# Two-block kernel: where the mixers' weights get their lower parts

## The chip, the cores and the metric

The kernel runs on 1 core of one Trainium2 chip. The metric is the device time of one execution in microseconds. A core has TensorE (PE, with its weight loads PEld), VectorE (DVE), ScalarE (ACT), GpSimd (POOL) and SyncE (SP), each with a queue of its own that it works through in order, and 16 DMA engines that move what any of the queues issues. Times of the profile are microseconds from the start of the span unless they are marked ns.

## The reference

Two transformer blocks follow each other on 512 tokens of width 1024, in float32. Each has an FFN, a mixer and a second FFN, with RMS norms and residuals around them. The first block prepends 16 meta tokens (528 columns).

```python
def first_block(...):
    h = concat(meta, x)
    h = h + 0.5 * rmsnorm(swiglu(rmsnorm(h, gn[0]), ffn_w_in[0], ffn_w_out[0]), gn[1])
    u = rmsnorm(h, gn[2])
    y = mlstm_mixer(u, a_w_in, a_conv_w, a_conv_b, a_gate_b, a_w_out)     # mixer A
    h = h + rmsnorm(y, gn[3])
    ...
def second_block(...):
    ...
    proj = rms_norm(h, mix_norm) @ w_in                                   # mixer B
    a = mla_group(c_q, c_kv, k_pe, pos_f, q_norm, w_uq, kv_norm, w_ukv)
    r = retention_group(r_q, r_k, r_v, r_g, pos_f, decay_fwd, decay_bwd)
    h = h + concat(a, r) @ w_o
    ...
```

Mixer A is an mLSTM: a causal convolution over queries and keys, gates, a scan, output gates and `a_w_out` (1024x1024). Mixer B joins a latent attention with 8 heads (`w_uq`, `w_ukv`) and a two-sided retention with 8 heads, and ends in `w_o` (1024x1024).

## The kernel before

Every float32 product is made of three: a matrix is split into an upper part `hi`, rounded to float32r, and a lower part `lo` = value - `hi`; TensorE multiplies hi by hi, hi by lo and lo by hi and adds them up in PSUM (`mm`, L484). Activations are split as they come (`split`, L463 to L470); weights are split when they have been loaded.

The class `Weights` runs the weights' way. SP loads raw weights into two buffers `raw0` and `raw1` in turn (`load`, L85 to L99). `pump` (L107) takes the next unit, 128 partitions by 1024 columns as a rule, gives it a free slot (a pair of tiles `hi`, `lo`), lets ACT write `hi` (L120) and lets `lo_engine` subtract it from the raw weights into `lo` (L121). When the last unit of a raw buffer is split, the load of the raw weights after the next ones is issued into it (L127 to L128); on the chip SP waits until the readers of the buffer are done. `take` hands units to TensorE in order, `free` and `release` give slots back and call `pump` again. In mixer A there are six slots, in mixer B four.

`lo_engine` is DVE in the FFNs and POOL in the two mixers: set to POOL at L1129 (mixer A, after its first items) and L1339 (mixer B), and back to DVE in `Bridge.tail` and near the end of mixer B. In mixer A a unit is one head's or one pair's columns of `a_w_in`, then `a_w_out` in raw loads of two units each (256 columns, so a unit reads eight runs of 512 bytes per partition). In mixer B a unit is 128 columns of `w_in_2` or, once for each pair of heads, the `w_uq` and `w_ukv` columns of `add_mla`, which come in four pieces (96, 16 and 16 columns of four blocks, and 256 columns). `w_o_2` follows.

Around this the mixers run items: an item multiplies one unit with all tokens, and `evac` brings the sums out of PSUM with DVE. Steps of the attention are laid between an item's matmuls (`run_mm`, `run_item`). In mixer A, `done_gate` runs a chain on DVE (L1005 to L1027: a polynomial at L1015, scans, an exponential on ACT), `item_qk.done` the convolution (three taps at L1067, a last product at L1070), `masked` scales the scores (L1177) and splits them, and `divided` makes the quotient (L1205 to L1212). In mixer B, `newton` (L380 to L387) makes the inverse roots of the norms, `Rms.to` the diagonal matrices (L450) that TensorE turns into rows (L451), `item_rqk` the rotated queries and keys (L1525 to L1536), and `ret_attn` multiplies them (L1589).

POOL has other work in the mixers: the masks of mixer A (L1158), copies and one subtraction for queries and keys (L1080, L1081, L1539), and a few DMAs. In the FFNs POOL issues accumulating DMAs of 256 KB (L95), which add weights in HBM to a raw tile.

Of the kernel before, what the change touches and what calls it, by code (L numbers as in the profile page):

```python
# [8 lines left out]
F32 = mybir.dt.float32  # L9
F32R = mybir.dt.float32r  # L10
I32 = mybir.dt.int32
ACTF = mybir.ActivationFunctionType
ALU = mybir.AluOpType
# [50 lines left out]
class Weights:  # L64
# [42 lines left out]
    def pump(self):  # L107
        nc = self.nc
        while self.n_split < len(self.subs):
            r, make, half = self.subs[self.n_split]  # L110
            if self.hold and self.raws[r][2] and self.raws[r][1] == 5:
                break
            idle = self.idle_halves if half else self.idle
            if not idle:
                break
            slot = idle.pop(0)
            self.dma(r + 1)
            unit, splits = make(self.raw_tiles[r], slot.hi, slot.lo)
            for ho, lw, src in splits:
                nc.scalar.copy(out=ho, in_=src)  # L120
                self.lo_engine.tensor_tensor(out=lw, in0=src, in1=ho.bitcast(F32), op=ALU.subtract)  # L121
            unit.slot = slot
            self.units.append(unit)
            self.n_split += 1
            self.raws[r][1] -= 1
            if self.raws[r][1] == 0:
                del self.raw_tiles[r]  # L127
            if self.raws[r][1] == 0:  # L128
                self.dma(r + 3)
            if self.raws[r][2] and self.raws[r][1] == 2 and self.n_raw == r + 2 and self.raws[r + 2][2]:  # L130
                self.load(r + 2, True)
# [88 lines left out]
def two_blocks(ctx: ExitStack, tc, d, out):  # L220
    nc = tc.nc
    pe, act, dve, pool = nc.tensor, nc.scalar, nc.vector, nc.gpsimd

    def open_pool(name, bufs=1, **kw):
        cm = tc.tile_pool(name=name, bufs=bufs, reuse_waits="tile", **kw)
        return cm, cm.__enter__()
# [30 lines left out]
    def cut(t, k, sl):  # L257
        return t[:, k, sl[0]:sl[0] + sl[1]]


    W = Weights(nc, rawp)
# [316 lines left out]
    def run_lead(items, br, keep=None):  # L578

        sa, sb = br.sa, br.sb  # L580
        us = [W.take(it.units) for it in items]
        if keep:
            W.reserve(keep, 1)
        accA = [[ps("accA")[0:u.hi.shape[2], 0:sa[1]] for u in uu] for uu in us]

        pairs = [(u, p) for uu, aa in zip(us, accA) for u, p in zip(uu, aa)]
        step = br.first
        for i in range(0, len(pairs), step):
            for k in ALLK:
                for u, p in pairs[i:i + step]:  # L590
                    mm([(p, sa)], u, [k], NORMED, last=KD - 1)
                if i == 0 and k == br.ks[0]:
                    br.pres[sa].flush(1)
                    br.post_b()
                elif i == 0 and k == br.ks[1]:
                    br.set_rp(sb)
        br.pres[sa].compact()
        for c in range(KD):
            br.chunk(c, sb)
        held = []  # L600
        for i, it in enumerate(items):
            bank = ps("accB")
            accB = [bank[0:u.hi.shape[2], n * sb[1]:(n + 1) * sb[1]] for n, u in enumerate(us[i])]
            for n, (u, p) in enumerate(zip(us[i], accB)):
                for k in ALLK:
                    mm([(p, sb)], u, [k], NORMED, last=KD - 1)
                    br.pres[sb].flush(KD - 1 - k)
                if i == 0 and n == 0:
                    br.pres[sa].set_r()
                    for x, a in zip(items, accA):  # L610
                        x.evac(sa, a)
            held.append(accB)
            if i == 0:
                br.pres[sb].compact()
            if i == 2:
                br.pres[sb].set_r()
            while i >= 2 and held:
                x = items[i + 1 - len(held)]
                x.evac(sb, held.pop(0))
                if x.done:  # L620
                    x.done()
                W.free(x.units)
# [503 lines left out]
    make = {"k": lambda n: item_qk("k", n), "q": lambda n: item_qk("q", n), "v": item_v, "o": item_o}  # L1126
    lead = [Item(1, ev_gate, done_gate)] + [make[k](n) for k, n in order[:3]]
    run_lead(lead, br)
    W.lo_engine = pool  # L1129
    for k, n in order[3:6]:  # L1130
        run_item(make[k](n), AB)
    cm_s, sp = open_pool("mixs")
# [203 lines left out]
    close_pool(cm_w2)  # L1336


    W.lo_engine = pool  # L1339
    cm_b, bp = open_pool("mixb")  # L1340
    hsp = drp.tile([P, KD, SEQ], F32, name="hsp")
    pool.dma_start(out=hsp, in_=h[:, :, NM:TT])
# [415 lines left out]
    for sl in halves:  # L1758
        for c in range(KD):
# [14 lines left out]
            src = cut(h, c, sl)  # L1774
# [57 lines left out]
```

## Time and profile before

| | |
|---|---|
| median of 3 runs | 2091.21 us (2089.55 to 2098.18) |
| profiled execution | 2091.01 us, span 2089.1 us, mean granted clock 0.99 |
| PE busy | 2006.3 us (96%) |
| DVE busy | 1549.0 us (74%) |
| ACT busy | 1027.4 us (49%) |
| POOL busy | 326.9 us (16%) |
| HBM read | 230.53 MB |

The share of busy time is an average over stages with different limits, and a busy TensorE is not one at its peak, since ends of matmuls are modelled. A row of a timeline gives the start, the duration, the engine, the line, the operation, what is written and read, and in brackets the idle time of the engine just before, with what ended it.

### The profile page before, as it was taken

What the parts mean: (1) busy time and instruction counts of PE and PEld (TensorE: products, weight loads), DVE (VectorE), ACT (ScalarE), POOL (GpSimd) and SP (SyncE); (2) the same over time, 40 slices, a digit from 0 to 9 for tenths busy, and PEclk for the clock granted to TensorE, in tenths of its full rate; (3) what the DMA queues carried; (4) which work ended last, traced back from release to release, by engine and by line L of the source; (5) the groups of instructions that cost most, each with busy time, mean ns of one, the idle gap of its engine ahead of it and who ended that gap; (6) DMA issues with size and microseconds to landing.
All of it is one profiled execution on the core that took longest, in us unless ns stands there. A gap on an engine that the chain in (4) does not pass through costs nothing.

```text
span 2089.1 us, 34858 instructions
## 1 busy us (share of the span) xinstructions
PE 2006.3 (96%) x13583; PEld 1840.6 (88%) x13583; DVE 1549.0 (74%) x2949; ACT 1027.4 (49%) x1973; POOL 326.9 (16%) x290
## 2 busy tenths in 40 slices
PE   8999999989999999999999999998999999999998
PEld 8999999988889989989998988987777778898998
DVE  6848477787886767758777775877888877676684
ACT  5445255445555445436443543654666643353462
POOL 0011020034430002011000201103222100010200
PEclk9999999999999999999999999999999999999999
DMA  6357565222223327567532766733112153475661
GB/s 186 96 111 152 147 140 135 72 77 81 87 81 110 79 79 156 145 137 146 162 80 77 154 152 137 148 118 104 47 47 61 41 141 100 107 158 133 147 151 55
DMA packets 387851, 237.01 MB, mean 113 GB/s; under 512 B 10427, under 2 KB 383926, under 8 KB 387686
## 3 DMA queue, kind: packets, MB, share of 16 engines
q1 hardware_dynamic: 317446, 192.94, 31.4%
q0 software_dynamic: 69680, 40.62, 14.1%
q8 instruction: 106, 1.74, 0.3%
q10 hardware_dynamic: 560, 1.24, 0.2%
q14 instruction: 59, 0.48, 0.1%
HBM read 230.53 MB, written 4.23 MB: 112 GB/s over the span
## 4 chain that ended last, share of the span: by engine, by line
PE 77%; DVE 12%; ACT 5%; issue 3%; POOL 1%; DMA 1%; ACTq 0%; POOLq 0%; DVEq 0%
PE dn L484 23%; PE sa L696 17%; PE acc L484 11%; PE sc L696 8%; PE sb L696 4%; PE accB L484 3%; PE accA L484 3%; PE wo L484 2%; DVE wlo L121 1%; DVE accF L1206 1%; ACT sqFalse L753 1%; PE p L419 1%; PE ro L1604 1%; ACT whi L120 1%; DVE cv L1067 1%
## 5 line engine op out<-in xcount | busy, mean ns | idle before, releaser
L120 ACT CAST whi<-raw 128x1024 fp32r<-128x1024 f32 (+3 forms) x500 | 392.8, 801 | 360.0 <-PE dn L484 163.2
L121 DVE TENSOR_TENSOR wlo<-raw,whi 128x512 fp32r<-128x512 f32 (+2 forms) x456 | 402.3, 905 | 112.9 <-ACT whi L120 110.4
L484 PE MATMUL dn<-gh,whi 128*128 128x256 f32 (+2 forms) x908 | 277.6, 326 | 0.5 <-ACT gh L465 0.5
L484 PE MATMUL dn<-gl,whi 128*128 128x256 f32 (+2 forms) x908 | 277.7, 326 | 0.0
L484 PE MATMUL dn<-gh,wlo 128*128 128x256 f32 (+2 forms) x908 | 276.9, 325 | 0.0
L484 PE MATMUL acc<-nh,whi 128*128 128x512 f32 (+2 forms) x600 | 196.4, 361 | 8.9 <-DVE y L1212 3.9
L484 PE MATMUL acc<-nl,whi 128*128 128x512 f32 (+2 forms) x600 | 192.0, 355 | 0.0
L484 PE MATMUL acc<-nh,wlo 128*128 128x512 f32 (+2 forms) x600 | 191.6, 354 | 0.0
L484 PEld LDWEIGHTS dn<-gh,whi 128*128 128x128 f32 x908 | 163.0, 188 | 16.5 <-ACT gh L465 0.7
L484 PEld LDWEIGHTS dn<-gh,wlo 128*128 128x128 f32 x908 | 163.1, 188 | 15.0
L484 PEld LDWEIGHTS dn<-gl,whi 128*128 128x128 f32 x908 | 163.0, 188 | 15.1
L696 PE MATMUL sa<-nh,whi 128*128 128x256 f32 (+1 forms) x488 | 142.5, 292 | 24.9 <-ACT sqFalse L753 24.9
L696 PE MATMUL sc<-nh,wlo 128*128 128x256 f32 (+1 forms) x488 | 137.4, 282 | 0.0
L696 PE MATMUL sa<-nh,wlo 128*128 128x256 f32 (+1 forms) x488 | 137.3, 281 | 0.0
L696 PE MATMUL sc<-nh,whi 128*128 128x256 f32 (+1 forms) x488 | 137.2, 281 | 0.0
L696 PE MATMUL sa<-nl,whi 128*128 128x256 f32 (+1 forms) x488 | 137.1, 281 | 0.0
L696 PE MATMUL sc<-nl,whi 128*128 128x256 f32 (+1 forms) x488 | 137.0, 281 | 0.0
L484 PEld LDWEIGHTS acc<-nh,whi 128*128 128x128 f32 (+1 forms) x600 | 108.1, 194 | 25.9 <-DVE z L1054 4.5
L696 PEld LDWEIGHTS sa<-nh,whi 128*128 128x128 f32 x488 | 91.8, 188 | 34.9 <-ACT sqFalse L753 34.7
L484 PEld LDWEIGHTS acc<-nh,wlo 128*128 128x128 f32 (+1 forms) x600 | 107.0, 194 | 15.5
L484 PEld LDWEIGHTS acc<-nl,whi 128*128 128x128 f32 (+1 forms) x600 | 106.8, 193 | 13.9
L95 POOL DMA_DIRECT2D raw<-in_ffn_w_up x32 | 41.1, 1285 | 455.9 <-DMA raw<-in_ffn_w_up 245.4
(492 smaller groups left out, 5569.5 us busy)
## 6 DMA issues: line engine op xcount, KB each, us to landing
raw<-in_ffn_w_in SPq DMA_DIRECT2D x56, 512.0 KB, 3.9
raw<-in_ffn_w_gate SPq DMA_DIRECT2D x44, 512.0 KB, 3.7
raw<-in_ffn_w_in SPq DMA_DIRECT2D x64, 256.0 KB, 3.2
raw<-in_ffn_w_out SPq DMA_DIRECT2D x16, 1024.0 KB, 7.7
raw<-in_ffn_w_up SPq DMA_DIRECT2D x64, 256.0 KB, 3.3
raw<-in_ffn_w_down SPq DMA_DIRECT2D x16, 1024.0 KB, 7.2
raw<-in_a_w_in SPq DMA_DIRECT2D x18, 512.0 KB, 3.6
rawx<-in_ffn_w_in SPq DMA_DIRECT2D x32, 256.0 KB
```

The lines of the kernel that those rows point to most:

```text
L95: self.nc.gpsimd.dma_start(out=dst(t), in_=src, accum_op=ALU.add)
L120: nc.scalar.copy(out=ho, in_=src)
L121: self.lo_engine.tensor_tensor(out=lw, in0=src, in1=ho.bitcast(F32), op=ALU.subtract)
L419: pe.matmul(self.p1[:, self.n:self.n + 2], lhsT=src[:, o:o + P], rhs=ones[:, 0:2], start=True, stop=True)
L484: pe.matmul(p, lhsT=w[:, k], rhs=cut(x, k, sl), start=(k == 0 and j == 0), stop=(k == last and j == 2))
L696: pe.matmul(acc, lhsT=w[:, 4 * i + k], rhs=x[:, k], start=start and k == 0 and j == 0, stop=k == 3 and j == 2, skip_group_check=not start)
L753: last = act.copy(out=m3, in_=o.a)
L1067: dve.scalar_tensor_tensor(out=v, in0=z[:, t0 + j:t0 + j + n], scalar=col(V_CW + 8 * j + c), in1=v, op0=ALU.mult, op1=ALU.add)
L1206: dve.reciprocal(out=dn, in_=dn)
L1604: pe.matmul(o[i], lhsT=vt_[:, i, j], rhs=s_[i, j][b], start=(j == 0 and b == 0), stop=(j == 3 and b == 1))
```

## The change

In the two mixers the lower part is no longer subtracted by POOL. ACT writes the negated upper part into `lo` (a copy with scale -1, rounded to float32r as `hi` is), and a DMA that POOL's queue issues adds the raw weights to it, from SBUF to SBUF. The FFNs, the tail of mixer A and the end of mixer B keep DVE's subtraction. The places at which the way is switched are the same as before.

```diff
@@ in Weights.pump
             for ho, lw, src in splits:
                 nc.scalar.copy(out=ho, in_=src)
-                self.lo_engine.tensor_tensor(out=lw, in0=src, in1=ho.bitcast(F32), op=ALU.subtract)
+                if self.lo_engine is None:
+                    nc.scalar.activation(out=lw, in_=src, func=ACTF.Copy, scale=-1.0)
+                    nc.gpsimd.dma_start(out=lw.bitcast(F32), in_=src, accum_op=ALU.add)
+                else:
+                    self.lo_engine.tensor_tensor(out=lw, in0=src, in1=ho.bitcast(F32), op=ALU.subtract)
@@ in mixer A, after run_lead
-    W.lo_engine = pool
+    W.lo_engine = None
@@ at the head of mixer B
-    W.lo_engine = pool
+    W.lo_engine = None
```

## Rows read from the trace of the kernel before

**Rows 1.** The page's first line.

```profile
span 2089.1 us, 34858 instructions
```

**Rows 2.** The table of stretches: start and end, length, then busy time and instructions of PE, PEld, DVE, ACT and POOL, the granted clock, the DMA engines' share and GB/s. The first two lie in mixer A, the last at the end of mixer B.

```profile
436.00:460.00 24.00, 17.07 (x116) 15.90 (x115) 23.46 (x23) 8.08 (x14) 11.63 (x8) 0.86 0.24 67
...
520.00:600.00 80.00, 72.82 (x475) 67.78 (x474) 65.64 (x78) 40.23 (x81) 36.59 (x43) 0.94 0.27 82
...
1620.00:1662.00 42.00, 39.63 (x212) 32.28 (x211) 35.52 (x80) 30.31 (x63) 8.67 (x6) 1.00 0.10 29
```

**Rows 3.** TensorE's waits: who waited for whom, us in total, times, the longest. First those of 436 to 640 us, then those of 1410 to 1662 us.

```profile
PE aT L1035 <- DVE y L1024: 6.9, 1, 6.9
PE acc L484 <- DVE y L1212: 3.9, 2, 2.0
PE acc L484 <- DVE z L1054: 3.7, 3, 1.2
...
PE rs L1589 <- DVE rk L1536: 7.8, 3, 3.0
PE p L451 <- DVE dg L450: 5.9, 4, 3.9
```

**Rows 4.** Instructions of line L121 (the subtraction) on POOL: duration in ns min/median/max, first and last start, and forms.

```profile
L121 POOL TENSOR_TENSOR wlo<-raw,whi x44: 319/2389/2661, 436.7 to 1643.9; 128x1024 fp32r<-128x1024 f32 x32, 128x64 fp32r<-128x64 f32 x6, 128x384 fp32r<-128x384 f32 x3, 128x256 fp32r<-128x256 f32 x3
...
L121 POOL TENSOR_TENSOR wlowide<-raw,whiwide x13: 320/2395/2537, 445.0 to 1657.8; 128x1024 fp32r<-128x1024 f32 x9, 128x64 fp32r<-128x64 f32 x2, 128x384 fp32r<-128x384 f32 x1, 128x256 fp32r<-128x256 f32 x1
```

**Rows 5.** Two lines of DVE with all their instructions in the kernel: duration in ns min/median/max, first and last start, and forms.

```profile
L1070 DVE SCALAR_TENSOR_TENSOR cv<-z,cv x8: 654/708/2867, 436.7 to 570.5; 128x528 f32<-128x528 f32 x4, 128x512 f32<-128x512 f32 x4
...
L380 DVE TENSOR_SCALAR nw_y<-nw_v x20: 104/169/2401, 35.0 to 2081.6; 128x2 int32<-128x2 int32 x13, 128x4 int32<-128x4 int32 x4, 128x3 int32<-128x3 int32 x3
```

**Rows 6.** DVE's timeline in mixer A, two instructions of the convolution that stand in the chain of the gates.

```profile
436.74 2.87 DVE L1070 SCALAR_TENSOR_TENSOR cv<-z,cv 128x528 f32<-128x528 f32 x1
...
444.99 2.98 DVE L1067 SCALAR_TENSOR_TENSOR cv<-z,vec,cv 128x512 f32<-128x512 f32 x1
```

**Rows 7.** The timelines of POOL and DVE in the first FFN: a DMA issue of POOL's, and a DVE instruction beside it with two inputs in SBUF.

```profile
163.86 1.77 POOL L95 DMA_DIRECT2D rawx<-in_ffn_w_in  x1
...
164.80 0.43 DVE L719 SCALAR_TENSOR_TENSOR sqFalse<-b,sqFalse 128x264 f32<-128x264 f32 x1 [0.55 <-ACT b L718]
```

**Rows 8.** The timelines of ACT, POOL, DVE and PE in one period of mixer A.

```profile
533.44 1.05 ACT L120 CAST whi<-raw 128x1024 fp32r<-128x1024 f32 x1
534.83 0.53 ACT L465 CAST sh<-w 128x400 fp32r<-128x400 f32 x1 [0.34 <-DVE w L1177]
...
535.25 2.38 POOL L121 TENSOR_TENSOR wlo<-raw,whi 128x1024 fp32r<-128x1024 f32 x1
...
535.39 2.68 DVE L466 TENSOR_TENSOR sl<-w,sh 128x400 fp32r<-128x400 f32 x1 [0.32 <-ACT sh L465]
...
543.19 0.61 DVE L466 TENSOR_TENSOR sl<-w,sh 128x432 fp32r<-128x432 f32 x1
...
544.81 0.39 PE L484 MATMUL acc<-nh,whi 128*128 128x256 f32 x1 [1.25 <-DVE z L1054]
```

**Rows 9.** The timelines of DVE and PE at the start of mixer B.

```profile
1416.19 2.40 DVE L380 TENSOR_SCALAR nw_y<-nw_v 128x4 int32<-128x4 int32 x1
...
1436.05 3.44 DVE L466 TENSOR_TENSOR mk<-t,mk 64x512 fp32r<-64x512 f32 x2
...
1439.84 1.01 PE L451 MATMUL p<-dg,ones 128*128 128x128 f32 x3 [3.92 <-DVE dg L450]
```

**Rows 10.** The timelines of ACT, DVE and PE where the third pair's keys are rotated in mixer B.

```profile
1546.77 1.05 ACT L120 CAST whi<-raw 128x1024 fp32r<-128x1024 f32 x1 [1.29 <-PE mkv L1430]
...
1548.36 2.47 DVE L1529 TENSOR_TENSOR t<-t 128x512 f32<-128x512 f32 x1
1550.76 0.67 DVE L466 TENSOR_TENSOR mk<-mkv,mk 64x512 fp32r<-64x512 f32 x1
...
1550.87 1.26 ACT L1535 CAST rk<-t 64x512 fp32r<-64x512 f32 x2 [1.77 <-DVE t L1529]
...
1552.89 0.47 PE L1589 MATMUL rs<-rq,rk 128*128 128x512 f32 x1 [2.95 <-DVE rk L1536]
```

**Rows 11.** ACT's timeline in the attention of the last pair in mixer B.

```profile
1642.80 1.05 ACT L120 CAST whi<-raw 128x1024 fp32r<-128x1024 f32 x1
1643.87 0.59 ACT L465 CAST ph<-mpT 128x512 fp32r<-128x512 f32 x1
```

**Rows 12.** The DMA views: the time from issue to landing of all DMAs of line L95 (POOL's accumulating ones), the queue of POOL's DMAs (packets, MB, share of 16 engines), and two loads of SP's (count, KB each, median us to landing).

```profile
DMA to landing us min/median/max: 4.4/5.7/8.1
...
q0 software_dynamic: 69680, 40.62, 14.1%
...
raw<-in_a_w_in SPq DMA_DIRECT2D x18, 512.0 KB, 3.6
...
raw<-in_w_uq SPq DMA_DIRECT2D x4, 192.0 KB, 2.4
```

**Rows 13.** The timelines of ACT and SP around the reload of a raw buffer in mixer B: the split of the unit that lies in it, the reload, and the split of the next unit from it.

```profile
1488.18 1.05 ACT L120 CAST whi<-raw 128x1024 fp32r<-128x1024 f32 x1
...
1491.81 0.37 SPq L99 DMA_DIRECT2D raw<-in_w_uq  x1
...
1498.87 0.51 ACT L120 CAST whi<-raw 128x384 fp32r<-128x384 f32 x1 [2.59 <-PE acc L484]
```

## Prediction

> **What bounds the kernel now.** The page comes first: the span is 2089.1 us, and the profiled run took 2091.01 us, so 1.9 us lie outside the span and the run stands 0.2 us under the median of 2091.21 [rows 1]. The edit acts in two stretches only, mixer A (436 to 640 us) and mixer B (1410 to 1662 us), so the next view is the table of stretches. TensorE is nearly full there, but less than in the FFNs: in 436 to 460 it has 17.07 of 24 us, and the granted clock is 0.86; in 520 to 600 it is 0.94 [rows 2]. The third view is what TensorE waits for: in A 6.9 us for the gate's scan chain and 3.9 + 3.7 us for PSUM evacuations, in B 5.9 us for the diagonals of the norms and 7.8 us for the rotated keys. All of these are DVE's [rows 3]. So the mixers are bound by a DVE chain that hands over to TensorE late, and the question is what makes DVE late.
>
> The fourth view gives that. POOL subtracts 41 whole units of 128x1024 here, 2.4 us each, and 16 smaller pieces [rows 4]. A DVE instruction that meets one of them takes much longer: the tap of L1070 takes 0.71 us at the median and 2.87 at most, the Newton seed of L380 0.17 and 2.40 [rows 5], and the long ones stand under POOL's subtracts [rows 6, 8, 9]. DVE waits out POOL's instruction.
>
> **What is removed.** POOL's 57 subtracts go, and with them the stretches. A DMA issue from POOL doesn't do the same: beside an issue of 1.77 us DVE's two-input instruction takes 0.43 us [rows 7], so I take the returned DVE time whole; if an issue still held DVE, see the fourth rival.
>
> A1, the gate chain: L1070 gives back 2.87 - 0.71 = 2.2, L1067, of the same form, 2.98 - 0.71 = 2.3; 4.4 us of the 6.9 us wait [rows 3, 5, 6].
> A2, the evacuations: 3.9 + 3.7 = 7.6 us in five waits, 1.5 us each. One is worked through: the cast `hi` ends at 534.49, the cast `sh` starts at 534.83, DVE's subtract runs 535.39 to 538.07 and TensorE waits 1.25 us at 544.81 with DVE full in between [rows 8]. Afterwards the negated copy ends at 535.5, `sh` at 536.0, and the subtract, some 0.6 long (0.61 at 543.19, where POOL does nothing), at 536.6: 1.4 us earlier, so this wait goes whole. The others have less slack on ACT; I take three quarters, 5.7 us (ends 2 and 7.6).
> A3, the clock: the granted share lost in 436 to 600 is 0.14 x 24 + 0.06 x 80 = 8 us in the two stretches shown [rows 2]. I take 3 of the 8, as the idle times get shorter but don't go (ends 0 and 8).
> B1, the first norms: DVE gets back 2.40 - 0.17 = 2.2 and, for the two L466 (0.67 each when plain), 3.44 - 1.34 = 2.1 us, in front of a wait of 3.9 us (and a smaller one just before it) [rows 5, 9, 10]. Five negated copies fall in the same stretch; I take 3.5 (ends 1.5 and 4.6).
> B2, the next norm's seed, the rest of the 5.9 us: 1.0 (ends 0 and 1.3) [rows 3].
> B3, the keys, three times: L1529 gives back 1.8 (2.47 against 0.67 for the next one of 512 columns). But the copy that starts at 1546.77 is followed by its negated one until 1548.8, and only then come the query's cast and the key's two (1.26 for two); the keys' lower parts end near 1551.5, the wait ended at 1552.89 [rows 10]: 1.4 less, and 0.8 where the wait is shorter; 3.6 in all (ends 1.2 and 7).
>
> **What is added on ScalarE.** Each `hi` cast of 1024 columns takes 1.05 us [rows 8, 11]; the negated copy has its size, source and type, so I take 1.05 (0.96 where the two overlap; below nothing it can't be, since an instruction is added). 41 x 1.05 + 16 small ones (4 x 1.4) = 49 us of ACT. In A ACT is about half busy, and the cost is inside A1 and A2. In B it isn't hidden at four places, the splits inside the attention of the pairs: in the last of them the cast ends at 1643.85, `ph` starts at 1643.87, and none of the gains above lies there. ACT is busy 30.3 of the last 42 us [rows 2, 11]. 4 x 0.95 + 0.9 for the last split = 4.7 us longer (ends 0 and 6).
>
> **What is added on POOL and the DMA queue.** 57 issues take the place of the subtracts. The nearest are the accumulating issues of the FFNs, 256 KB; one takes 1.77 us [rows 7], against 2.4, so the queue behind POOL (masks, the queries' casts) is not later. Their time from issue to landing is 4.4 / 5.7 / 8.1 us. Queue 0 spends 14.1% of 16 engines' 2089.1 us on 69680 packets, 68 ns a packet [rows 12]; 512 KB in 512-byte runs are 512 packets more, 32 an engine, 2.2 us. Estimate of the landing: 5.7 + 2.2 = 7.9 us (ends 4.4 and 2 x 8.1 = 16.2, as no row shows an addition from SBUF to SBUF).
>
> The Trainium skill's "DMA: Bandwidth & Descriptors", section "Anatomy of one DMA", fits 2.0 us + bytes / 436e3; for 512 KB that would be 3.2 us, and the sum would be 3 us better; the rows of accumulating DMAs are far above it, and I keep them.
>
> Who waits for the landing? Not TensorE: a split fills the slot just freed, so its lower part is due when the units of the other slots are done, three in B and five in A; the splits of rows 13 are two units and 10.7 us apart, so three are some 16 us. Hidden. SP's reload of the raw buffer waits for it, and then the next split on ACT. B4: in B the load of `w_uq` goes out at 1491.81, 3.6 us after the cast began at 1488.18, and its split starts at 1498.87, when TensorE frees the slot [rows 13]. Afterwards: 1488.18 + 2.1 + 7.9 = 1498.2, + 0.4 issue + 2.4 landing [rows 12, 13] = 1501.0, so ACT stands 2.1 us, with the casts of the retention queued behind it. This comes twice (pairs 2 and 3); I take 1.5 each, 3 us, as these source rows are contiguous (ends 0 and 21). In A 21 of the 41 units are split in 204 us, and a buffer serves every second one, every 19 us on the mean; 2.1 + 7.9 + 3.6 = 13.6 [rows 12] fits.
>
> **The sum.** A: -4.4 - 5.7 - 3.0 = -13.1. B: -3.5 - 1.0 - 3.6 + 4.7 + 3.0 = -0.4. Together -13.5 from 2091.0: **2077 us**, 6 us either way for the places chosen.
>
> **Rivals.** (1) DVE's time comes back in full and ACT hides its copies: A -4.4 - 7.6 - 8, B -4.6 - 1.3 - 5.4 (1.8 x 3) with no costs: -31, **2060**. For it: all large waits of the mixers are for DVE [rows 3]. Against: casts stand back to back on ACT in B [rows 11].
> (2) ACT pays it back: the negated copy stands in front of every chained cast, A1 stays, A2 gives 2, the clock nothing, B -2.7 + 4.7 + 3: about -1.5, **2090**. For it: rows 10 and 11. Against: ACT's idle time in rows 8.
> (3) The reload takes the wait's place: if the landing is long, SP loads late and ACT stands at its next split. Each us over 7.3 costs 2 us more in B, and from 19 - 5.7 = 13.3 each costs up to 10 in A (once for each pair of splits); at 13.4 us the gain is gone, at 15 us it is 15.4 + 17 - 13.5 = 19 us slower, **2110**. For it: 41 transfers twice as large as any in rows 12. Against: the longest shown is 8.1.
> (4) The change doesn't free DVE, because POOL's issue holds it as the subtract did: 4.7 + 3 + some 3 us on ACT in A, **2102**. Against: rows 7.
> (5) DVE holds up POOL's issue, the other way round. If an issue could go on only while DVE is idle, 14.4 of 80 us [rows 2], its 1.77 us [rows 7] would take 9.9; 21 of them put 21 x 7.5 = 158 us on POOL in A in place of the subtracts, and POOL, busy 0.46 of the time now [rows 2], would need 94 + 158 = 252 of 204 us: 48 us slower there, **2125**. Against: the issue in rows 7 is 1.77 long with DVE at work beside it. The Trainium skill's "SBUF — State Buffer", section "SBUF: two separate sides", states this rule for DVE's two-port modes: descriptors of a DMA issued from GpSimd can't be written meanwhile (620 ns become 3100 there). It speaks against this change; rows 7 show no such issue.
>
> **How the numbers follow.** Forecast 0.42, rival 1 0.19, rival 2 0.20, rival 3 0.10, rival 4 0.06, rival 5 0.03. A measurement here can tell some 0.5%, 10.5 us, from no change: faster is under 2080.7, slower over 2101.7. Of the forecast's own span (2071 to 2083) seven tenths are under the line: 0.29, with rival 1 0.48, and a tenth of rival 2 on this side: 0.50. Slower: rivals 3 and 5 and half of rival 4: 0.16. The rest, 0.34, is the same. The range reaches from a little under rival 1 to rival 4, 2057 to 2103; it leaves out rivals 3 and 5 and what is beyond rival 1, some 0.18.
>
> **What would show it.** In the changed profile L1070 and L380 must have their maxima near their medians; the wait for the scan chain must be under 3 us; the keys' wait under 2 us. A wait of ACT's L120 for a raw tile at the two places of B shows B4. If the landing is over 13 us, or DVE's instructions are still stretched beside POOL's issues, the forecast is wrong. ACT's order of instructions may be laid out anew, which could move either way the 4.7 us.

## The result, and the profile of the changed kernel

The changed kernel takes **2058.44 us** (median of 4 runs, 2057.64 to 2064.95); the kernel before, run on the same chip, takes 2094.07 us (2089.55 to 2098.18). The ratio of their means is 0.9837, with a 95% interval of 0.9806 to 0.9869: faster, by 1.6%. The forecast was 2077 us and a gain of 13.5 us; between the spans of the two profiled executions the gain is 32.3 us. It is the time of the first rival (2060 us), and the range (2057 to 2103 us) held it by 1.4 us.

The page of the changed kernel, its first line:

```profile
span 2056.8 us, 34973 instructions
```

The table of stretches of the changed kernel (columns as in [rows 2]; the first two are the same stretches as there, the last is the end of mixer B, which now comes some 32 us earlier):

```profile
436.00:460.00 24.00, 22.15 (x155) 20.07 (x153) 21.01 (x31) 12.48 (x20) 9.24 (x11) 0.98 0.53 117
520.00:600.00 80.00, 78.88 (x509) 71.85 (x508) 59.19 (x80) 51.25 (x94) 30.32 (x43) 1.00 0.76 149
1590.00:1632.00 42.00, 38.75 (x197) 31.11 (x197) 35.90 (x79) 32.02 (x62) 5.87 (x5) 0.96 0.45 72
```

TensorE's busy time in the first two goes from 17.07 to 22.15 of 24 us and from 72.82 to 78.88 of 80, and the granted clock from 0.86 and 0.94 to 0.98 and 1.00. ScalarE has 11 us more in the second, and DVE 6.5 us less, although the same 80 us now hold more of the mixer. At the end of B the clock is 0.96 where it was 1.00.

TensorE's waits in the changed kernel, first in mixer A (436 to 640 us), then in mixer B (1385 to 1640 us), against [rows 3]:

```profile
PE acc L488 <- DVE y L1216: 1.1, 2, 0.7
PE sc L1176 <- POOL q L1084: 1.1, 1, 1.1
PE sc L1176 <- POOL ql L1085: 0.8, 1, 0.8
PE p L455 <- DVE dg L454: 0.5, 1, 0.5
...
PE mo L1501 <- DVE pl L470: 5.0, 4, 1.5
PE p L455 <- DVE dg L454: 2.2, 3, 0.9
PE ro L1608 <- ACT rsh L469: 2.1, 3, 1.0
PE mo L1501 <- ACT ph L469: 1.2, 2, 0.7
```

In A the scan chain's wait (6.9 us) and that for `z` (3.7) are gone, and that for `y` is 1.1 us; two waits for POOL's work on the queries, 1.9 us, have come. In B the wait for the rotated keys (7.8 us) is gone and that for the norms fell from 5.9 to 2.2; but the waits in front of the attention's values (`mo`, `ro`) are 8.3 us together, where the kernel before has 0.9.

Two lines of DVE in the changed kernel (duration in ns min/median/max), the answer to [rows 5]:

```profile
L1074 DVE SCALAR_TENSOR_TENSOR cv<-z,cv x8: 691/701/709, 439.0 to 552.3; 128x528 f32<-128x528 f32 x4, 128x512 f32<-128x512 f32 x4
...
L384 DVE TENSOR_SCALAR nw_y<-nw_v x20: 104/169/293, 36.3 to 2049.3; 128x2 int32<-128x2 int32 x13, 128x4 int32<-128x4 int32 x4, 128x3 int32<-128x3 int32 x3
```

The maxima were 2867 and 2401 ns. **The stretch** of DVE in a mixer, here and below, is the sum over its instructions of the duration less the shortest one of the same line, written tile and shape, worked out from the trace and good to about 1 us; A is counted from its first projection to the next FFN's first matmul, B likewise. It falls from 37.0 to 7.4 us in A and from 27.1 to 5.4 in B. TensorE's idle time falls from 21.0 to 5.6 us in A and from 18.5 to 11.8 in B, and the mixers get shorter from 281.2 to 258.6 and from 304.8 to 293.5 us: 22.6 + 11.3 = 33.9 us. Of these, 22.1 us are idle time of TensorE and the rest is busy time that got shorter: the time at a granted clock of 0.5 (1.2 of 2.4 GHz) falls from 23.9 to 10.2 us in A and from 10.2 to 3.4 us in B. The rest of the kernel is as long as before to within 2 us.

ScalarE's, POOL's and DVE's timelines of the changed kernel in one period of mixer A, as in [rows 8]:

```profile
529.51 1.03 ACT L120 CAST whi<-raw 128x1024 fp32r<-128x1024 f32 x1
530.45 1.05 ACT L122 ACTIVATE wlo<-raw 128x1024 fp32r<-128x1024 f32 x1
531.40 0.60 ACT L469 CAST sh<-w 128x512 fp32r<-128x512 f32 x1
...
531.80 1.59 POOL L123 DMA_DIRECT2D wlo<-raw  x1 [1.89 <-ACT wlo L122]
...
532.04 0.69 DVE L470 TENSOR_TENSOR sl<-w,sh 128x512 fp32r<-128x512 f32 x1 [1.74 <-ACT sh L469]
```

Here DVE's subtraction, with two inputs in SBUF, runs inside POOL's DMA issue and takes 0.69 us; inside POOL's subtraction it took 2.68. The cast `sh` starts right behind the negated copy, and TensorE doesn't wait for it here.

### The profile page after: what moved, and what is told of

It is laid out like the page before. It is cut to its first block, busy times and chain, and to the rows that moved or that the text cites. A ratio compares the mean times of both kernels' runs of the same rounds, so it can differ in the third digit from the quotient of the medians.

```text
span 2056.8 us, 34973 instructions
## 1 busy us (share of the span) xinstructions
PE 1996.8 (97%) x13583; PEld 1835.5 (89%) x13583; DVE 1495.4 (73%) x2949; ACT 1068.1 (52%) x2030; POOL 283.0 (14%) x290
## 3 DMA queue, kind: packets, MB, share of 16 engines
q0 software_dynamic: 95040, 63.69, 21.8%
## 4 chain that ended last, share of the span: by engine, by line
PE 82%; DVE 7%; ACT 5%; issue 3%; DMA 2%; POOL 1%; ACTq 0%; POOLq 0%; DVEq 0%; SPq 0%
PE dn L488 25%; PE sa L700 18%; PE acc L488 12%; PE sc L700 9%; PE sb L700 4%; PE accB L488 3%; PE accA L488 3%; PE wo L488 2%; ACT sqFalse L757 1%; PE p L423 1%; ACT whi L120 1%; PE ro L1608 1%; DVE wlo L125 1%; DMA raw<-in_w_uq 1%; DMA raw<-in_ffn_w_down 1%
## 5 line engine op out<-in xcount | busy, mean ns | idle before, releaser
L488 PE MATMUL acc<-nh,whi 128*128 128x512 f32 (+2 forms) x600 | 191.0, 353 | 1.1 <-DVE y L1216 1.1
L95 POOL DMA_DIRECT2D raw<-in_ffn_w_up x32 | 41.1, 1284 | 455.3 <-DMA raw<-in_ffn_w_up 236.4
```

Source lines behind the costliest of these rows:

```text
L95: self.nc.gpsimd.dma_start(out=dst(t), in_=src, accum_op=ALU.add)
L488: pe.matmul(p, lhsT=w[:, k], rhs=cut(x, k, sl), start=(k == 0 and j == 0), stop=(k == last and j == 2))
```

## The experiments

All of them are built from the kernel before or from the changed kernel; the medians stand beside runs of the kernel before on the same chip (2091.4 to 2092.2 us).

**Mixer A alone.** The changed kernel with the second switch left as it was:

```diff
@@ at the head of mixer B
-    W.lo_engine = None
+    W.lo_engine = pool
```

> Only mixer A has the new path; mixer B keeps POOL's subtracts. Theory (T1): POOL's two-input subtract makes DVE stand, and the gain is DVE's time returned where the subtracts were. By the two profiles the stretch from A's first projection to the next FFN is 22.6 us shorter with the change, so this run should be 21 to 24 us under the kernel before, some 2070, with B's stretch as long as before (249 us from its first projection to its last). Rival (order): the instructions were laid out anew over the whole program, and part of the gain hangs on that; then the two halves alone don't add up to the whole (33 us), and A alone may give anything between 13 (my forecast's sum) and 33.

Measured: 2068.13 us, ratio 0.9889 (0.9875 to 0.9902). A takes 256.5 us, B 305.6.

**Mixer B alone**, the other switch:

```diff
@@ in mixer A, after run_lead
-    W.lo_engine = None
+    W.lo_engine = pool
```

> Only mixer B has the new path; mixer A keeps POOL's subtracts. T1: the stretch of B was 11 us shorter with the change, so some 10 us under the kernel before, 2083, and with the run that has only A changed it adds up to the whole, 33 us. My forecast for B was 0.4 us, as ScalarE's copies and the reload were to cost 7.7; if they cost that in B alone, this run is within 2 us of the kernel before. Rival (order): does not add up with the run of A alone.

Measured: 2079.98 us, 0.9941 (0.9928 to 0.9953); A 281.5 us, B 291.2. The two gains, 23.6 and 11.7 us, add up to 35.3; the whole is 35.6 between the medians. So each mixer's gain comes without the other's, and B, for which I had forecast 0.4 us, gains 12.

**DVE writes the lower parts.**

From the kernel before, at both switches:

```diff
-    W.lo_engine = pool
+    W.lo_engine = dve
```

> DVE writes the lower parts itself in both mixers: 57 subtracts of at most 1.22 us each (some 26 us of DVE time in A, 28 in B), nothing on POOL, no negated copy, no DMA. T1: POOL's subtracts stretched DVE's own instructions by some 32 us in A and 25 in B, so DVE has to do about as much as before, 20 to 30 us more than with the change; between the two kernels, 2075 to 2090. Rival (POOL's queue is what was late: masks and casts behind 2.4 us subtracts): POOL's queue is empty here too, so the whole gain comes, 2060. Rival (DVE only loses): slower than before, over 2094.

Measured: 2066.51 us, 0.9882 (0.9869 to 0.9896): 8 us below the range of my theory. A takes 258.9 us, as with the change, although DVE does every subtraction itself; B takes 298.8. The stretch is 8.4 and 5.9 us. Taking the subtraction off POOL is most of the gain, wherever it goes. Between the medians the way through ScalarE and the DMA is 8 us better still; of these the profiled executions place 0.3 us in A and 5.3 in B.

**POOL copies in place of the subtraction.** From the kernel before:

```diff
-                self.lo_engine.tensor_tensor(out=lw, in0=src, in1=ho.bitcast(F32), op=ALU.subtract)
+                if self.lo_engine is nc.vector:
+                    nc.vector.tensor_tensor(out=lw, in0=src, in1=ho.bitcast(F32), op=ALU.subtract)
+                else:
+                    for _ in range(2):
+                        nc.gpsimd.tensor_copy(out=lw, in_=src)
```

> The kernel before, with POOL's subtract replaced by two copies of the raw weights into the lower part, one input each, about as long together (2 x 1.2 us); it leaves the subtraction of the upper part out. POOL's queue is as full as before, ScalarE and the DMA queues have nothing more. T1: a one-input operation doesn't make DVE stand, so DVE's time comes back and the time is that of the changed kernel or a little less (what the copies on ScalarE and the DMAs cost), 2050 to 2062. Rival (queue): the gain came from POOL's queue being shorter; then the time stays at 2090 to 2094. Rival (any POOL operation holds DVE): also 2090 to 2094, and the trace shows DVE's instructions of 2 to 3 us beside the copies.

Measured: 2065.93 us, 0.9875 (0.986 to 0.989), between the expectations. POOL's and DVE's timelines in that run:

```profile
1472.04 2.49 POOL L125 CAST wlo<-raw 128x1024 fp32r<-128x1024 f32 x2 [5.18 <-PE mkv L1434]
...
1472.17 1.46 DVE L1533 TENSOR_TENSOR t<-t 128x512 f32<-128x512 f32 x1
1473.55 0.67 DVE L470 TENSOR_TENSOR mk<-mkv,mk 64x512 fp32r<-64x512 f32 x1
```

DVE stands beside a copy with one input too (the same line took 2.47 us in [rows 10]), but only until the first of the two copies ends; then it gets through. So "two-input" was wrong in my theory. The next one is that the length of a single POOL instruction counts, which the run after this tests. The stretch is 21.4 + 17.5 us, and POOL is as busy as before (93 and 66 us of instructions against 96 and 66), so it isn't POOL's queue either.

**The subtraction in quarters.** From the kernel before, four subtractions of a quarter of the columns each:

```diff
-                self.lo_engine.tensor_tensor(out=lw, in0=src, in1=ho.bitcast(F32), op=ALU.subtract)
+                n = 1 if self.lo_engine is nc.vector else 4
+                ax = 1 if len(src.shape) == 2 or src.shape[1] % n == 0 else 2
+                k = src.shape[ax] // n
+                for i in range(n):
+                    c = (slice(None),) * ax + (slice(k * i, k * i + k),)
+                    self.lo_engine.tensor_tensor(out=lw[c], in0=src[c], in1=ho[c].bitcast(F32), op=ALU.subtract)
```

> The kernel before, with each of POOL's subtracts in the mixers cut into four of a quarter of the columns (some 0.6 us each). POOL's work is the same or a little more, with two inputs as before; ScalarE and the DMA queues have nothing more. The run with one-input copies showed that the number of inputs isn't it: DVE stood beside a copy too, until the copy ended, and got through between two copies. Theory (T1b): any POOL instruction on SBUF holds a DVE instruction whose operands are all in SBUF, until the POOL instruction ends, so the price of a meeting is the length of one POOL instruction; cut into quarters, a meeting costs at most 0.6 us in place of 2.2, the 62 us that DVE is stretched by in the two mixers fall to 15 to 30, and the time is 2060 to 2070. Rival (POOL's queue): POOL is as busy as before or more, so 2088 to 2095. Rival (two inputs hold DVE for the whole series of four): also 2088 to 2095, with DVE's instructions of over 2 us still in the trace.

Measured: 2073.27 us, 0.9912 (0.9899 to 0.9925), 19 us faster with the same subtractions on the same engine. POOL's instructions add up to 122 + 95 us, 55 more than before, so the rival of the queue falls. TensorE's, DVE's and ScalarE's instructions stand in both mixers in the very order of the kernel before, so no new order is behind these 19 us. The line of [rows 5] in that run, and some of TensorE's waits (A, then B):

```profile
L1075 DVE SCALAR_TENSOR_TENSOR cv<-z,cv x8: 654/708/1197, 436.4 to 564.0; 128x528 f32<-128x528 f32 x4, 128x512 f32<-128x512 f32 x4
```

```profile
PE aT L1040 <- DVE y L1029: 5.7, 1, 5.7
PE acc L489 <- DVE z L1059: 3.7, 3, 1.2
...
PE rs L1594 <- DVE rk L1541: 1.7, 3, 0.6
```

The maximum is 1.20 us in place of 2.87. The gain falls short of the expected 22 to 32 us, since DVE now meets more pieces: the stretch is 24.5 + 17.1 us, and the scan chain still costs 5.7 us.

**POOL's work put back.** The changed kernel, with an operation of POOL's behind each issue:

```diff
                     nc.gpsimd.dma_start(out=lw.bitcast(F32), in_=src, accum_op=ALU.add)
+                    h = ho.bitcast(F32)
+                    nc.gpsimd.tensor_tensor(out=ho, in0=h, in1=h, op=ALU.add)
```

> The changed kernel, and behind each DMA issue POOL adds the upper part to itself in place, a two-input operation of the subtract's size (2.4 us); it doubles the upper parts of the mixers' weights. ScalarE's copies and the DMAs stay as they are. T1b: DVE stands again beside 41 operations of 2.4 us, and the stretch is back at 55 to 65 us: the gain is lost, 2085 to 2105 (POOL is busier than in the kernel before by its issues, so rather the upper half). Rival (the gain comes from the new order of the instructions): most of the gain stays, under 2075.

Measured: 2082.33 us, 0.9956 (0.9944 to 0.9968). 24 us of the gain are lost, with ScalarE's copies and the DMAs kept: A goes from 258.6 to 271.4 us, B from 293.5 to 304.1. In B TensorE, DVE and ScalarE keep the very order of the changed kernel, in A TensorE does. The operation took 1.89 us, not 2.4, and the stretch is 21.8 + 18.4 us, less than the 55 to 65 that I expected; so the time lies just under the expected range. TensorE doesn't wait for POOL in its list of waits.

**ScalarE's copy twice.**

```diff
                     nc.scalar.activation(out=lw, in_=src, func=ACTF.Copy, scale=-1.0)
+                    nc.scalar.activation(out=lw, in_=src, func=ACTF.Copy, scale=-1.0)
```

> The changed kernel with the negated copy on ScalarE written twice, 57 instructions and some 49 us of ScalarE more. My forecast's terms: 4.7 us at the splits inside the attention of the pairs, and the reload of the raw buffer 1.05 us later, 3 us more at most: 2063 to 2066. Theory that ScalarE's copies are hidden (my first rival): at most 2 us, 2058 to 2061. My second rival (ScalarE pays it back in both mixers): over 2070.

Measured: 2061.30 us, 0.9852 (0.9835 to 0.9869): 2.9 us for 49 us of ScalarE, and the intervals don't tell even that from nothing. At this median the copies are hidden but for some 6% of their time. The profiled execution has no cost in B, where I had placed it (292.1 us against 293.5); A is 4.7 us longer.

**The negated copy on DVE.**

```diff
-                    nc.scalar.activation(out=lw, in_=src, func=ACTF.Copy, scale=-1.0)
+                    nc.vector.tensor_scalar(out=lw, in0=src, scalar1=-1.0, scalar2=None, op0=ALU.mult)
```

> The changed kernel with the negated copy written by DVE (one input, some 0.9 us for 1024 columns by the 0.48 us of L1478 for 512) and not by ScalarE. Theory: ScalarE's copies cost B the new waits in front of the values of the latent attention (mo) and of the retention (ro), 8.3 us together in the changed kernel; without them these waits fall under 3 us and B gains some 5 us, while DVE's 25 us in each mixer cost A nothing and B 2 to 4: 2055 to 2059. Rival (B is bound by DVE and not by ScalarE): half of what the kernel with DVE's subtracts lost against the changed one, 2061 to 2065.

Measured: 2065.14 us (2061.14 to 2073.67), 0.9881 (0.9865 to 0.9898). The theory fails; the time is at the upper edge of the rival's. The profiled execution is the fastest of the five, 4 us under the median, so its waits may be on the low side. TensorE's waits in B in that run:

```profile
PE mo L1501 <- DVE pl L470: 5.9, 4, 1.9
...
PE ro L1608 <- ACT rsh L469: 1.0, 1, 1.0
```

ScalarE writes no negated copy here, and the waits for the values are 6.9 us; with the copies written twice they are 4.1 (3.0 + 0.5 for `mo`, 0.6 for `ro`). So they follow neither from the copies being there nor from their number.

**Each DMA twice.**

```diff
                     nc.gpsimd.dma_start(out=lw.bitcast(F32), in_=src, accum_op=ALU.add)
+                    nc.gpsimd.dma_start(out=lw.bitcast(F32), in_=src, accum_op=ALU.add)
```

> The changed kernel with each accumulating DMA of the lower parts issued twice (the lower parts then hold the raw weights once too often). POOL has 57 issues of 0.9 to 2.5 us more, and the raw buffer is free a landing later, some 10 us after the cast in place of 5. T1b: issues don't hold DVE, so within 5 us of the changed kernel, 2056 to 2064, as far as the reload stays hidden. Rival (POOL's queue): masks and casts wait behind the issues, half of the gain lost, 2070 or more. My third rival (the reload takes the wait's place; by its terms each us over a landing of 7.3 costs 2 us in B): 2064 to 2072, with waits of ScalarE for the raw tiles of over 4 us in the pairs of B.

Measured: 2129.76 us, 1.0187 (1.0166 to 1.0207), far beyond the ranges; only the queue's rival ("2070 or more") was open to that side. What POOL and ScalarE waited for in A (430 to 690 us) in that run:

```profile
POOL wlo L124 <- DMA wlo<-raw: 67.1, 15, 6.6
```

```profile
ACT w L1167 <- POOL w L1163: 39.0, 13, 7.8
ACT whi L120 <- DMA raw<-in_a_w_in: 17.0, 8, 5.3
```

The second DMA adds to the tile that the first one writes, so it stands on POOL's queue until the first has landed, and the masks of A wait behind it. ScalarE waits for raw tiles at the same time, so this run alone can't say which of the two costs the 71 us. The next two runs separate them.

**Two issues without the wait.** The DMA in two halves:

```diff
-                    nc.gpsimd.dma_start(out=lw.bitcast(F32), in_=src, accum_op=ALU.add)
+                    ax = 1 if len(src.shape) == 2 or src.shape[1] % 2 == 0 else 2
+                    k = src.shape[ax] // 2
+                    for i in range(2):
+                        c = (slice(None),) * ax + (slice(k * i, k * i + k),)
+                        nc.gpsimd.dma_start(out=lw[c].bitcast(F32), in_=src[c], accum_op=ALU.add)
```

> The changed kernel with each accumulating DMA issued in two halves, 57 issues more on POOL (0.9 to 2.5 us a whole one). In the run with each DMA issued twice, the second issue stood on POOL until the first had landed (idle time of some 87 us in A, 71 in B); here the halves don't depend on each other, so POOL only issues longer. Theory (T1b): an issue doesn't hold DVE, and POOL's queue has room: stretch of DVE's instructions 11 us as in the changed kernel, time within 4 us of it, 2056 to 2062. Rival (POOL's queue, with its issue time, is what counts): some 45 us more on POOL, masks and casts later, 2068 or more.

Measured: 2058.79 us, 0.9846 (0.9833 to 0.9859), the time of the changed kernel. POOL's instructions rise from 74 to 116 us in A and from 58 to 146 in B, and the stretch stays at 8.0 + 5.4. An issue doesn't hold DVE, and POOL has room.

**The raw weights later.** Each load of the mixers issued twice into the same buffer:

```diff
-            for dst, src in loads[k:]:
-                self.nc.sync.dma_start(out=dst(t), in_=src)
+            for _ in range(2 if self.lo_engine is None and not more else 1):
+                for dst, src in loads[k:]:
+                    self.nc.sync.dma_start(out=dst(t), in_=src)
```

> The changed kernel with every raw load of the mixers loaded twice into the same buffer, the second behind the first: the raw weights arrive some 2.5 to 4 us later, POOL, DVE and the accumulating DMAs as before. My third rival's mechanism (ACT stands at its next split, each us later costs 2 us in B): 2062 to 2068, with ACT's waits for raw tiles up from 11.6 us in B by 10 or more. Theory that the reload has slack: within 3 us, 2056 to 2061, though ACT's waits may grow. If the reload is what made the run with doubled DMAs 71 us slower, A must lose too, and the time must be over 2080.

Measured: 2088.89 us, 0.9987 (0.9976 to 0.9997): 30 us of the gain gone, more than either expectation. A takes 273.7 us, B 309.9. The second load stands until the first has landed: in SP's list of waits 13 times and 49.3 us in all for `a_w_in`, 15 times and 45.7 us for `w_in`, so 3 to 4 us each, and 4.7 to 6.7 us each for the loads of 1024 KB (`w_o`, `a_w_out`). A stretch of A, and ScalarE's timeline ahead of B's second pair:

```profile
460.00:520.00 60.00, 52.16 (x306) 46.89 (x305) 34.33 (x50) 36.91 (x69) 19.77 (x36) 0.87 0.77 193
```

```profile
1468.28 1.05 ACT L121 CAST whiwide<-raw 128x1024 fp32r<-128x1024 f32 x1 [3.36 <-DMA raw<-in_w_in]
1469.35 0.58 ACT L470 CAST ph<-mpT 128x512 fp32r<-128x512 f32 x1
```

ScalarE stands 3.36 us at the split, and the attention's cast `ph`, for which TensorE waits 2.30 us at 1471.14, stands behind it. With the work of POOL, DVE and ScalarE unchanged, some 3 to 7 us of lateness at each reload cost 15 us in A and 16 in B. The doubled loads also fill the DMA engines (0.91 of 520 to 600 us, against 0.76), and the lower parts land after 5.6 us at the median in place of 5.2; this part isn't separated. So the third rival's mechanism is real and dearer than I had put it, and the changed kernel stands close to it. It also makes the reload a part of the 71 us of the run with each DMA twice; how these divide between the reload and the masks was not tried.

**Keys and queries on DVE.** The last two-input operations of POOL in A go to DVE:

```diff
-                (dve if i else pool).tensor_tensor(out=low[i][rows] if kind == "q" else st[i][rest, 0:n],
+                dve.tensor_tensor(out=low[i][rows] if kind == "q" else st[i][rest, 0:n],
                                                    in0=v[rows], in1=st[i][rows, 0:n].bitcast(F32), op=ALU.subtract)
```

> The changed kernel with the last two-input operations of POOL in mixer A, the first half of the lower parts of keys and queries (8 of 1.3 to 1.45 us), on DVE, which already writes the other half. By the trace DVE's half takes 1.28 us beside POOL's and 0.69 alone, so DVE has 8 x (2 x 0.69 - 1.2) = 1.4 us more and the pair ends at the same time; POOL is free 11 us longer. T1b: 0 to 3 us faster than the changed kernel, 2055 to 2059. Rival (DVE has no time to give in A): 2 to 5 us slower, 2060 to 2063.

Measured: 2056.27 us, 0.9833 (0.9821 to 0.9846). The stretch in A falls from 7.4 to 4.8 us, and the time is 2 us under the changed kernel's, which the intervals can't tell from no difference.

## Why the prediction was right, and where its sizes were off

**The cause** is the forecast's: POOL's subtracts made DVE stand, DVE handed over late, and TensorE waited and lost clock. Four runs carry it. With POOL just as busy or busier but its single instructions shorter, more than half of the gain comes (19 us with quarters, 26 with copies); with POOL's work put back into the changed kernel, 24 us of it go; with more issues on POOL nothing happens. Over these runs the two mixers together take 586.0 us at a stretch of 64.1 us, 565.0 at 41.6 (quarters), 559.2 at 38.9 (copies) and 552.1 at 12.8 (the change): the first third of the stretch was worth nearly its own length, 21.0 us for 22.5, the rest half of it, 12.9 us for 28.8. The sum of the stretch doesn't fix the time, though. With POOL's work put back A takes 271.4 us at 21.8 us of stretch, with the copies 262.4 at 21.4: in the first the scan chain's wait is 5.1 us, in the second 2.1, which suggests that it also counts which instruction is held. And at nearly the stretch of the quarters (40.2 us) the run with POOL's work put back takes 575.6 us, 10.6 more, all of it in B, where the waits for the values are 6.4 us against 1.4 and the time at half clock is longer.

**A1 and A2** were nearly right. Forecast 4.4 of the 6.9 us of the scan chain's wait: all of it went. Forecast 5.7 of 7.6 for the evacuations: 6.5 went (1.1 are left).

**A3, the clock, is the term that was most mis-sized in A.** I took 3 of 8 us since the idle times would "get shorter but don't go". In the two stretches of [rows 2] the granted share lost is now 0.02 x 24 + 0.00 x 80 = 0.5 us, so 7.7 us came back: the idle times did go. Over the whole of A the granted share lost falls from 11.9 to 5.1 us. With 6.9 + 6.5 + 7.7 = 21.1 us the terms make up nearly all of A's 22.6. This term moves between executions: in the run of mixer A alone, with the same code in A, the clock is full all through A, which takes 256.5 us.

**B1 and B2** said 4.5 us, and the wait for the norms' diagonals gave back 3.7; the stretch from B's first projection to its first latent projection is 6.1 us shorter (40.3 to 34.1).

**B3, the keys, failed in its premise.** I had the negated copy stand between the weights' cast and the keys' casts. In the changed kernel it doesn't; DVE's, ScalarE's and TensorE's timelines where the third pair's keys are rotated (counterparts in [rows 10]):

```profile
1518.12 0.68 DVE L1533 TENSOR_TENSOR t<-t 128x512 f32<-128x512 f32 x1
...
1518.77 1.05 ACT L120 CAST whi<-raw 128x1024 fp32r<-128x1024 f32 x1
1519.72 1.25 ACT L1539 CAST rk<-t 64x512 fp32r<-64x512 f32 x2
...
1522.46 1.06 ACT L122 ACTIVATE wlo<-raw 128x1024 fp32r<-128x1024 f32 x1
...
1521.19 0.47 PE L1593 MATMUL rs<-rq,rk 128*128 128x512 f32 x1
```

The keys' casts follow the weights' cast at once, the negated copy comes 3.7 us after it, and TensorE starts without a wait. With the orders of the kernel before (the run with quarters) the same wait fell to 1.7 us: 6.1 of 7.8 came from DVE alone, where I had 3.6. Whether the rest hung on the pieces that DVE still met or on the order isn't shown.

**ScalarE's 4.7 us** were the wrong cost: waits of 8.3 us did appear in the attention of the pairs, where I had looked for them, but that is luck. They stay at 6.9 without any negated copy on ScalarE, and 49 us more on ScalarE cost the kernel 2.9, if anything. TensorE's instructions stand in another order in B than before, with some scores of the retention ahead of projections: with the order of before the waits for the values are 0.9 us (the kernel before), 1.4 (quarters) and 0.3 (POOL's copies); with the order of the changed kernel they are 8.3, 6.4 (POOL's work put back) and 7.4 (two issues); with other orders 4.1 (copies twice) to 12.4 (DVE's subtractions). So they go with the order. That it causes them is not shown, since no run changed it alone.

**The clock in B** had no term in the forecast, as I priced it in A alone. The granted share lost in B falls from 5.1 to 1.7 us, 3.4 us of the 11.3. With 3.7 for the norms, 7.8 for the keys and 2.3 for the waits for `mpT` (the transposes of the latent attention, L1488 before), less 7.4 more in front of the values, that makes 9.8; some 1.5 us aren't placed.

**B4, the reload**: 3.0 us were forecast at the pairs 2 and 3, with a landing of 7.9 us. The landing is shorter. DMAs of the changed kernel (count, KB each, median us to landing), and POOL's issues (ns):

```profile
wlo<-raw POOLq DMA_DIRECT2D x32, 512.0 KB, 5.2
...
raw<-in_w_uq SPq DMA_DIRECT2D x4, 192.0 KB, 3.9
```

```profile
L123 POOL DMA_DIRECT2D wlo<-raw x44: 857/1097/2559, 440.1 to 1613.8; - x44
```

Two parts of the sum 5.7 + 2.2 were too dear. Queue 0 moved 63.69 MB in 95040 packets, so the new transfers made 25360 packets for 23.07 MB, 910 bytes each on the mean and not the 512 that I had assumed. And the 5.7 us of transfers out of HBM don't hold from SBUF to SBUF: with contiguous columns, as at these pairs, 23 of 27 transfers of 512 KB land after 4.4 to 5.3 us. The Trainium skill's "DMA: Bandwidth & Descriptors", section "Anatomy of one DMA", gives 3.2 us as an estimate by its fit, too little by 2.0 for the median; the measurement lies between this and my 7.9 and decides. ScalarE's waits for raw tiles in B did come, at the other end of it, and ScalarE's timeline has the longest for `w_uq`:

```profile
ACT whi L120 <- DMA raw<-in_w_in: 7.4, 2, 4.7
...
ACT whi L120 <- DMA raw<-in_w_uq: 4.2, 2, 3.9
```

```profile
1399.52 0.51 ACT L120 CAST whi<-raw 128x384 fp32r<-128x384 f32 x1 [3.91 <-DMA raw<-in_w_uq]
```

All but 0.3 us of them lie in the first 50 us of B, where TensorE's list has no wait for ScalarE's casts, and not at the pairs 2 and 3. My rule "each us over 7.3 costs 2 us in B" was too mild by the run with late loads (16 us in B for some 3 to 5 us).

**The rivals.** The first came true: its -31 us against the -32.3 measured. Its conditions, that DVE's time comes back and that ScalarE hides its copies, are nearly what the stretch (64.1 to 12.8 us) and the doubled copies show. That its sum for B (-4.6 - 1.3 - 5.4) equals the measured 11.3 us is luck: the waits for norms and keys gave 11.5, the clock gave more, and new waits for the values took it back. The second (ScalarE pays it back) falls with the doubled copies. The third's landing of over 13 us didn't come; the longest is 11.7. The fourth and fifth (POOL's issue holds DVE, or DVE the issue) fall with the run of two issues; POOL's issues took 1.1 us at the median with DVE at work. The chance of 0.19 for the first rival was too small: the row that I set against it, casts back to back on ScalarE [rows 11], said nothing of who waits behind them. And seven tenths of 2071 to 2083 under a line of 2080.7 was eight tenths: 9.7 of 12 us.

## What to carry to other kernels

Where two engines get in each other's way, look at the length of the single instruction and at who is held behind it, and not at the sum of busy time: cutting POOL's subtractions into quarters gave 19 us with more work done, and DVE doing all of it by itself gave 25. When several waits in a stretch have one cause and the granted clock is down there, price the clock with the waits, since both went together here. And a step that is moved to a DMA must be followed to the buffer that it frees last: it had hardly any slack, and 3 to 7 us there were worth 30 us.

## What the runs showed of the hardware that I had not expected

A DVE instruction with its inputs in SBUF that meets a POOL operation, one input or two, ends a fixed time after POOL's ends, and the time hangs on DVE's form. POOL's and DVE's lines of the kernel before, the first beside [rows 10]:

```profile
1547.89 2.39 POOL L121 TENSOR_TENSOR wlo<-raw,whi 128x1024 fp32r<-128x1024 f32 x1 [0.61 <-ACT whi L120]
...
L1177 DVE SCALAR_TENSOR_TENSOR w<-sc,w x24: 544/598/692, 471.4 to 620.9; 128x512 f32<-128x512 f32 x8, 128x400 f32<-128x400 f32 x8, 128x432 f32<-128x432 f32 x8
```

The 2.47 us instruction of [rows 10] ends at 1550.83, 0.55 us after POOL's; it takes 0.67 to 0.69 alone. In the run with copies the first of the two copies ended at 1473.08 and DVE's instruction of 1.46 us at 1473.63, 0.54 us later. By the trace of the kernel before, 39 DVE instructions in the two mixers were held by 0.3 us or more, and all ended so: 0.55 to 0.57 us after POOL's for 512 or 528 columns, 0.43 to 0.44 for 400, 0.01 to 0.08 for small ones such as the norms'. DVE's instructions with an input in PSUM were not held: nine of L1177, which scales the scores, overlapped a subtraction and took 0.56 to 0.68 us, as long as its others. The Trainium skill's "SBUF — State Buffer", section "SBUF: two separate sides", states an exclusive lock between GpSimd's instructions and those of DVE with two inputs in SBUF or in a two-port mode, which whoever starts first holds for its whole instruction; the trace agrees, from DVE's side with the times above and from POOL's with the second copy, which started while DVE's instruction ran and took 1.38 us where the first took 1.04.

An issue of 512 KB from SBUF to SBUF took POOL 0.86 to 0.9 us where the raw columns are contiguous and about 1.56 where they come in runs of 512 bytes (the issue at 531.80 is one of these); the former had DVE at work for 59 to 100% of their time and didn't get longer with it. From issue to landing it took 4.4 to 5.3 us for 23 of the 27 with contiguous columns and 5.6 to 11.7 for the 14 with short runs. Two accumulating DMAs on one tile put the landing of the first, some 5 us, on POOL's queue.
